# Bias and mask of the second block's attentions: from TensorE products to an operand of the instruction that finds the maximum

## The chip, the cores and the metric

The kernel runs on one core of a Trainium2 chip. The metric is the device time of one execution in microseconds (us). TensorE (PE) multiplies, VectorE (DVE) and ScalarE (ACT) work element by element and read TensorE's results from PSUM banks, GpSimd (POOL) works on SBUF only and issues the stores, SyncE (SP) issues the loads. Each engine runs its own list of instructions in order.

## The reference, cut to what matters

Two blocks act on 512 tokens of 1024 features: a first block with attentions and 32 experts, then a second block of two layers. A layer has three branches, a gated sum of their projections and an output projection. Two branches are attentions of eight heads. Of these the scores matter here:

```python
# latent attention (96 features of a head): a token sees its own chunk of 64 and the earlier ones
s = jnp.einsum('bqhd,bkhd->bhqk', qi, k) * scale
mask = key_chunk[None, :] <= q_chunk[:, None]
s = jnp.where(mask[None, None], s, NEG_INF)
p = jax.nn.softmax(s, axis=-1)
...
# banded attention (64 features): the same keys here, since the band is 9 chunks and there are 8, and a bias by distance
dist = i[:, None] + pad - j[None, :]
bias = rel_table[:, jnp.clip(dist, -REL_CLIP, REL_CLIP) + REL_CLIP]
s = jnp.einsum('bqhd,bkhd->bhqk', qi, kb) * scale + bias[None]
s = jnp.where(valid[None, None, None, :], s, NEG_INF)
p = jax.nn.softmax(s, axis=-1)
```

## The kernel before, in words

Products in float32 accuracy are made of three products of split operands (`mm3`, L61 to L63: high by low, low by high, high by high). The order of the instructions is not written out: the program is traced in the order of the code and a scheduler with a model of the engines' times then orders each engine's list, within what the buffers allow.

A layer of the second block is `layer2`. After the norm and the spatial gating unit come the latent and then the banded attention. Each goes over two halves of four heads, in a half over the four query tiles i of 128 tokens, and in a tile over two pairs of heads. Tile i sees n = 128 (i + 1) keys, so n is 128, 256, 384 or 512. After each pair one of 40 fillers is traced (`filler`: a feature tile of u, z or the gates, 24 products of 512 columns into the one bank F, then ScalarE or ScalarE and VectorE empty it and GpSimd stores it).

A pair is `unit2`. For each of its heads `S_of` leaves the scores in one of four banks M. Then VectorE takes their maximum (L1093, n elements) and multiplies it by -scale (L1094, one element), ScalarE takes exp(scale * s - scale * max) from the bank into an SBUF tile P with the sum (L1096), VectorE inverts the sum (L1098) and scales P (L1099). There are four buffers of P. TensorE transposes P (L1107, bank T), the result is split into Ph and Pl, and three products per key tile with the values give O.

Mask and bias are products that are accumulated in the same bank:

- in the latent attention L1321 adds `quad` (128 x 128, bf16, NEG in its first 64 rows and last 64 columns) to the last 128 columns by a product with the identity, between the three products of queries and keys (L1320, L1322, L1323);
- in the banded attention L1373 and L1375 add the low and the high part of the bias, as products of a matrix that reverses the rows (`rev`) with `rsl` and `rsh`, where row p holds the bias table from position p on, and L1374 adds `quad`; then `mm3` adds queries by keys.

There are 64 pairs, 128 heads: in each layer 32 heads of either kind, 8 of each n. The tables are made once in the first block (`bias_tables`, L173 to L189): 16 rows of 640, split and stored in DRAM as Rh and Rl (40 KB each). Each half of the banded attention loads its four heads' rsh and rsl from there, 256 KB a head and part.

Of the kernel before, what the change touches and what calls it, by code (L numbers as in the profile page):

```python
# [28 lines left out]
# slots of an expert's list in the main path  # L29
NS = 96  # L30
# weight tiles of the experts that are loaded ahead of the router
# [3 lines left out]
def f(t):  # L35
    return t.bitcast(F32)


class Kern:
# [6 lines left out]
    def split(self, hi, lo, src, scale=None, eng=None):  # L46
        """hi = src rounded to float32r, lo = src - hi (exact)."""
        nc = self.nc
        if scale is None:
            self.last_act = nc.scalar.activation(hi, src, AF.Copy)  # L50
            self.last_dve = (eng or nc.vector).tensor_sub(lo, src, f(hi))  # L51
        else:
            nc.scalar.activation(hi, src, AF.Copy, scale=scale)
            self.last_dve = nc.vector.scalar_tensor_tensor(lo, src, scale, f(hi), op0=ALU.mult, op1=ALU.subtract)

    def mm3(self, out, pairs, start=True, stop=True):
        """out += sum over pairs ((ah, al), (bh, bl)) of a.T @ b in float32 accuracy."""
# [7 lines left out]
    def rstd(self, pool, ss, n, scale, name):  # L65
        """1 / sqrt(ss * scale + EPS): a first value from the exponent's bits and two Newton steps,
        their constants set for the smallest largest error (5e-7)."""
# [21 lines left out]
    def weight(self, src, nk, ncol, pools=None, q=None, parts=1, plan=()):  # L89
        """src: AP [nk*128, ncol] in DRAM. Returns per k tile (hi, lo) APs [128, ncol].  # L90
        plan: for the first chunks, the pools, what the split is to come behind, and the engine of the remainders."""
# [4 lines left out]
        for k0 in range(0, nk, q):  # L96
# [10 lines left out]
            if early:  # L107
                # behind the router's work on each engine
# [15 lines left out]
    def bcast(self, ap, n):  # L124
        """DRAM vector [n] on all partitions."""
        return bass.AP(tensor=ap.tensor, offset=ap.offset, ap=[[0, 128], [1, n]])

    def norm_T(self, i, x, gain, xh, xl, pool, keep=None):
        """Tile i of x [128, D], token-major -> x * rstd * gain, transposed and split."""
# [18 lines left out]
    def setup(self, ctx):  # L148
# [17 lines left out]
        # reversal of the rows  # L166
        rev = self.rev = c.tile([128, 128], F32R, name="rev")
        # diagonal tiles of the second block: a query's own chunk and the earlier ones are open
        quad = self.quad = c.tile([128, 128], BF, name="quad")
        nc.gpsimd.memset(quad, 0.0)  # L170
        nc.gpsimd.memset(quad[0:64, 64:128], NEG)

    def bias_tables(self, pool):  # L173
        """Bias tables of the banded attention, reversed and extended, over the scale of the scores, split:
        R[m] = 8 * tab[min(639 - m, 256)]"""
        nc = self.nc
        self.R = R = [self.dram.tile([2, 8, 640], F32, name=f"R{s}") for s in "hl"]
# [6 lines left out]
        rh, rl = pool.tile([16, 640], F32R, name="rh"), pool.tile([16, 640], F32R, name="rl")  # L184
        nc.gpsimd.tensor_scalar(rx, rx, 8.0, None, op0=ALU.mult)
        nc.gpsimd.tensor_copy(rh, rx)
        nc.gpsimd.tensor_sub(rl, rx, f(rh))
        self.st(R[0].rearrange("l h n -> (l h) n"), f(rh))
        self.st(R[1].rearrange("l h n -> (l h) n"), f(rl))  # L189

# [1 line left out]
    def probs(self, banks, nh, nk, scale, m, s, normal=False):  # L192
        """banks: scores in psum, [128, nh, nk * 128] each. Leaves the maxima in m and the sums of the exponentials
        in s ([128, heads]); returns per pair of heads and key tile the exponentials, over their sums if normal,
        transposed: (hi, lo) rhs [128, 2 heads, 128]."""
# [34 lines left out]
    def values(self, vs, pr, dst):  # L230
        """Sum over key tiles of values.T @ probs for a pair of heads -> dst [128 (head, dim), 128], whole or (hi, lo)."""
# [10 lines left out]
    def rope_tables(self, pool, cosap, sinap, gain, nrot, name):  # L242
        """A = C * gain, B = Sg * gain with its halves swapped; cos/sin given for the first nrot dims."""
# [18 lines left out]
    def headnorm(self, ps, nh, A, B, nrot, out, i):  # L262
        """ps: psum [128, nh*64] -> per-head rmsnorm and rotation, into out [128, nh, 64]."""
# [3 lines left out]
        # copied, so that the bank is free early  # L267
# [29 lines left out]
    def block1(self):  # L297
# [37 lines left out]
        # fillers after each query tile of the groups and of the dense branch  # L335
# [3 lines left out]
        def bank():  # L339
            """A psum bank of either pool, in turn."""  # L340
# [4 lines left out]
        def filler(n=1):  # L345
            """Feature tiles of the gates, as tanh(z / 2) = 2 sigmoid(z) - 1, kept in DRAM until the merge."""
# [16 lines left out]
        # masks over key tiles (earlier, own, later): 0 where allowed, NEG elsewhere;  # L363
        # it[p, c] = c - p, key - query = c - p + 128 * rel
# [15 lines left out]
        t = self.tmp.tile([128, 128], F32, name="mt", bufs=1)  # L380
        nc.gpsimd.iota(t, pattern=[[1, 128]], base=-127, channel_multiplier=1, allow_small_or_imprecise_dtypes=True)
        nc.vector.tensor_scalar(self.rev, t, 0.0, None, op0=ALU.is_equal)
        # keys, transposed and zero-padded: [pair, head of the pair, key]
# [34 lines left out]
        def scores(qh, ql, p, v, s, j0, j1, mk):  # L418
            """Scores of head s of query pair p, key pair v over key tiles j0..j1."""
# [8 lines left out]
        def scores_b(qh, ql, p, s):  # L428
            """The same for the dense branch; both halves of the partitions hold the keys."""
# [5 lines left out]
        # dense grouped-query branch; its keys and the inputs of the projections take the place of the groups' keys  # L435
# [5 lines left out]
        def combine(i):  # L441
            """Joins the dilation groups: weights exp(scale * (m_g - M)) / sum."""
# [68 lines left out]
        def dilated(g, tr):  # L511
# [21 lines left out]
            for i in range(NT):  # L533
# [5 lines left out]
                # outputs of the 8 heads, their maxima, their sums  # L539
# [32 lines left out]
        # a branch's first keys are projected before the last query tile of the one before  # L572
# [13 lines left out]
        # gates, branch projections, merge, output projection  # L586
# [30 lines left out]
        # rows of the accumulator that empty slots are added to  # L617
# [6 lines left out]
        for c, W in enumerate(Ws):  # L624
            banks = [bank() for _ in range(NT)] if c == 0 else None
            if c == 0:
                # weights outermost, so that those of the second half take their place early
# [18 lines left out]
    def route(self, pool):  # L646
        """Norm, router, top 4, ranks of the tokens in their experts' lists. Returns the work for half a tile."""
# [10 lines left out]
        # slots, less BIG: what the rank of a chosen token is compared with  # L658
# [5 lines left out]
        # rows of the accumulator that empty slots are added to  # L664
# [6 lines left out]
        # router weights times the norm's gain, rounded | remainders  # L671
# [6 lines left out]
        # per token: its number, less BASE; per (token, expert): its gate, rounded and remainder  # L678
# [11 lines left out]
        def half(i, c, x):  # L690
# [46 lines left out]
            # the first expert's slots before anything else  # L737
# [4 lines left out]
            for i, lt, tv, sel in todo:  # L742
                # gates: softmax of the four
# [15 lines left out]
    def onehot(self, pool, e, eng):  # L759
        """Tokens of the slots of an expert, one-hot: [token, tile, slot]."""  # L760
# [5 lines left out]
    def slots(self, bank, oh, V, vg, gi, gate):  # L766
        """Token of each slot (a spare row of its own for an empty one) and its gate, in columns: the work of either."""
# [22 lines left out]
    def moe_setup(self):  # L790
        """Constants of the experts, and their pool of raw weights."""
# [10 lines left out]
        # biases of all experts, rounded in rows 0-31, remainders in rows 32-63, their second half in rows 64-127  # L802
# [19 lines left out]
    def moe_early(self):  # L822
        """First weights of the first expert."""
# [689 lines left out]
```

## Time and profile before

| | us |
|---|---|
| median of three runs | 3157.68 |
| lowest and highest | 3156.82, 3165.53 |
| span of the profiled execution, first to last instruction | 3154.3 |
| its TensorE busy | 3020.5 |
| its VectorE busy | 2233.5 |
| its ScalarE busy | 1712.6 |
| its GpSimd busy | 629.4 |

The profile is of one execution, whose span is 3.4 us below the median of the runs; no other time is given for it. Matmuls are pipelined, so the record of one begins before that of the one ahead has ended: how long TensorE is taken by one is read from the distance of two starts, not from the duration.

### The profile page before, as it was taken

The page shows a single profiled execution, that of the slowest core. Times are in us where ns is not written, and L with a number is a line of the kernel's source. Part 1 is how long each engine was busy: PE and PEld are TensorE (multiplying, and loading weights), DVE is VectorE, ACT ScalarE, POOL GpSimd, SP SyncE. Part 2 cuts the span into 40 slices and gives each one's busy share as a digit, 9 for nine tenths or more (in the row PEclk, how much of TensorE's full clock was granted, in tenths as well). Part 3 has the DMA queues.
Part 4 walks back from the last instruction along what each step waited for, and adds up shares of the span by engine and source line. Part 5 has one row for each costly group of instructions (what it writes and reads, how often), then busy time and mean ns, then how long its engine had stood idle before and what let it go on. Part 6 is the DMA issues. An engine that isn't in the chain of part 4 may idle for free. (4 is left out here: it accounts for less than half of the span.)

```text
span 3154.3 us, 40478 instructions
## 1 busy us (share of the span) xinstructions
PE 3020.5 (96%) x14662; PEld 2327.0 (74%) x14662; DVE 2233.5 (71%) x3715; ACT 1712.6 (54%) x2535; POOL 629.4 (20%) x438
## 2 busy tenths in 40 slices
PE   8999899979999999999999998999999979999998
PEld 6898777766666666666666665878887868888876
DVE  7766587668888988888888987644455585545564
ACT  4645554336776777777777774434444234444432
POOL 1000011033324444444444002111101010111000
PEclk9999999979999999999999998999999989999999
DMA  5122232569999999999999995433435433334362
GB/s 160 61 62 68 88 105 77 181 228 321 350 347 328 338 344 343 343 346 344 343 340 350 344 346 155 128 112 104 122 111 191 150 104 118 113 114 116 102 235 91
DMA packets 407761, 648.48 MB, mean 206 GB/s; under 512 B 23028, under 2 KB 150532, under 8 KB 407556
## 3 DMA queue, kind: packets, MB, share of 16 engines
q1 hardware_dynamic: 387808, 585.73, 55.6%
q0 software_dynamic: 19168, 58.00, 6.1%
q8 instruction: 118, 1.93, 0.3%
q10 hardware_dynamic: 576, 2.10, 0.2%
q14 instruction: 91, 0.71, 0.1%
HBM read 596.16 MB, written 53.79 MB: 206 GB/s over the span
## 5 line engine op out<-in xcount | busy, mean ns | idle before, releaser
L51 DVE TENSOR_TENSOR wlo<-raw,whi 128x2048 fp32r<-128x2048 f32 (+3 forms) x636 | 1157.7, 1831 | 318.6 <-ACT whi L50 314.3
L50 ACT ACTIVATE whi<-raw 128x2048 fp32r<-128x2048 f32 (+3 forms) x646 | 973.2, 1531 | 211.0 <-PE M L63 104.1
L61 PE MATMUL G<-wlo,exh 128*96 128x512 f32 x1024 | 412.8, 403 | 1.8 <-DVE wlo L51 1.8
L63 PE MATMUL G<-whi,exh 128*96 128x512 f32 x1024 | 404.0, 394 | 0.0
L62 PE MATMUL G<-whi,exl 128*96 128x512 f32 x1024 | 403.8, 394 | 0.0
L763 POOL TENSOR_SCALAR poh<-i,rk 128x96 fp32r<-128x96 f32 x124 | 314.4, 2545 | 94.1 <-PE T L779 94.0
L61 PE MATMUL F<-xl,whi 128*128 128x512 f32 x768 | 311.3, 405 | 14.5 <-DVE fl L1199 7.0
L62 PE MATMUL F<-xh,wlo 128*128 128x512 f32 x768 | 304.5, 396 | 1.8 <-DVE wlo L51 1.8
L63 PE MATMUL F<-xh,whi 128*128 128x512 f32 x768 | 304.6, 397 | 0.0
L61 PE MATMUL M<-wlo,xh 128*128 128x512 f32 (+2 forms) x736 | 277.5, 379 | 7.0 <-DVE wlo L51 2.0
L62 PE MATMUL M<-whi,xl 128*128 128x512 f32 (+2 forms) x736 | 276.9, 377 | 0.7 <-DVE xl L51 0.7
L63 PE MATMUL M<-whi,xh 128*128 128x512 f32 (+2 forms) x736 | 273.3, 373 | 0.0
L61 PEld LDWEIGHTS G<-wlo,exh 128*96 128x96 f32 x1024 | 165.5, 162 | 81.2 <-issue 18.2
L63 PEld LDWEIGHTS G<-whi,exh 128*96 128x96 f32 x1024 | 165.5, 162 | 70.4
L62 PEld LDWEIGHTS G<-whi,exl 128*96 128x96 f32 x1024 | 165.9, 162 | 64.2 <-issue 1.2
L61 PE MATMUL Y<-wlo,ath 128*96 128x512 f32 x512 | 210.2, 411 | 2.6 <-POOL wlo L51 1.9
L62 PE MATMUL Y<-whi,atl 128*96 128x512 f32 x512 | 202.1, 395 | 0.0
L63 PE MATMUL Y<-whi,ath 128*96 128x512 f32 x512 | 201.6, 394 | 0.0
L61 PEld LDWEIGHTS F<-xl,whi 128*128 128x128 f32 x768 | 145.3, 189 | 53.4 <-DVE fl L1199 11.2
L61 PEld LDWEIGHTS M<-wlo,xh 128*128 128x128 f32 x736 | 164.7, 224 | 26.3 <-ACT kk L269 4.4
L62 PEld LDWEIGHTS M<-whi,xl 128*128 128x128 f32 x736 | 164.8, 224 | 15.5 <-DVE xl L51 1.4
L63 PEld LDWEIGHTS M<-whi,xh 128*128 128x128 f32 x736 | 164.6, 224 | 14.2 <-issue 0.2
(480 smaller groups left out, 5413.7 us busy)
## 6 DMA issues: line engine op xcount, KB each, us to landing
raw<-in_w_gate_up SPq DMA_DIRECT2D x256, 1024.0 KB, 6.4
raw<-in_w_down SPq DMA_DIRECT2D x124, 1024.0 KB, 7.1
raw<-in_w_in SPq DMA_DIRECT2D x154, 512.0 KB, 3.9
GZ<-fl POOLq DMA_DIRECT2D x80, 256.0 KB, 2.3
raw<-in_w_out SPq DMA_DIRECT2D x24, 512.0 KB, 4.0
raw<-in_w_branch SPq DMA_DIRECT2D x24, 512.0 KB, 4.4
gt<-GZ SPq DMA_DIRECT2D x48, 256.0 KB, 3.1
raw<-in_w_in SPq DMA_DIRECT2D x32, 256.0 KB, 2.9
```

The costliest lines, as they stand in the source:

```text
L50: self.last_act = nc.scalar.activation(hi, src, AF.Copy)
L51: self.last_dve = (eng or nc.vector).tensor_sub(lo, src, f(hi))
L61: nc.tensor.matmul(out, lhsT=ah, rhs=bl, start=start and i == 0, stop=False)
L62: nc.tensor.matmul(out, lhsT=al, rhs=bh, start=False, stop=False)
L63: self.last_mm = nc.tensor.matmul(out, lhsT=ah, rhs=bh, start=False, stop=stop and i == n - 1)
L763: eng.tensor_scalar(oh[:, i], self.i128[:, :NS], self.rk[:, i, e:e + 1], None, op0=ALU.is_equal)
```

## The change

The products with `quad`, `rev` and the tables go. VectorE's first instruction on the scores becomes one that reads the bank and a tile of the same shape in SBUF, writes P = -scale * (scores + tile) and, as a second output, the smallest of each row; ScalarE then takes exp(min - P) in place. The tile is `quad`, now 128 x 512 in float32, for the latent attention, and `rb`, the bias with NEG written into its masked corner by GpSimd, for the banded one. So that row q of `rb` can be loaded as a shifted row, the table is stored with 128 copies of each of its 16 rows: 16 x 128 rows of 640 numbers, 641 apart, which are 5.24 MB. A half of the banded attention loads 4 x 256 KB instead of 8 x 256 KB, into two buffers instead of one.

```diff
     def bias_tables(self, pool):
-        self.R = R = [self.dram.tile([2, 8, 640], F32, name=f"R{s}") for s in "hl"]
+        R = self.R = self.dram.tile([16, 128 * 641], F32, name="R")
...
-        rh, rl = pool.tile([16, 640], F32R, name="rh"), pool.tile([16, 640], F32R, name="rl")
         nc.gpsimd.tensor_scalar(rx, rx, 8.0, None, op0=ALU.mult)
-        nc.gpsimd.tensor_copy(rh, rx)
-        nc.gpsimd.tensor_sub(rl, rx, f(rh))
-        self.st(R[0].rearrange("l h n -> (l h) n"), f(rh))
-        self.st(R[1].rearrange("l h n -> (l h) n"), f(rl))
+        self.st(R.rearrange("h (q m) -> h q m", m=641)[:, :, :640], rx[:, None, :].to_broadcast([16, 128, 640]))
...
-    def unit2(self, S_of, nk, vs, scale):
+    def unit2(self, S_of, bias, nk, vs, scale):
...
             src = S_of(h)
-            nc.vector.reduce_max(nm[:, h:h + 1], src[:, :n], axis=AX.X)
-            nc.vector.tensor_scalar(nm[:, h:h + 1], nm[:, h:h + 1], -scale, None, op0=ALU.mult)
             pt = self.ptile.tile([128, 512], F32, name="P2", bufs=4)
-            nc.scalar.activation(pt[:, :n], src[:, :n], AF.Exp, bias=nm[:, h:h + 1], scale=scale,
+            nc.vector.tensor_tensor_reduce(pt[:, :n], src[:, :n], bias(h), scale=-scale, scalar=3e38,
+                                           op0=ALU.add, op1=ALU.min, accum_out=nm[:, h:h + 1])
+            nc.scalar.activation(pt[:, :n], pt[:, :n], AF.Exp, bias=nm[:, h:h + 1], scale=-1.0,
                                  accum_out=sp[:, h:h + 1])
...
+        quad = self.quad = c2.tile([128, S], F32, name="quad")
+        nc.gpsimd.memset(quad, 0.0)
+        nc.gpsimd.memset(quad[0:64, 448:], NEG)
...
-                            nc.tensor.matmul(b[:, :n], lhsT=qh[:, g], rhs=kl[:, g, :n], start=True, stop=False)
-                            nc.tensor.matmul(b[:, n - 128:n], lhsT=self.ident_b, rhs=self.quad, start=False, stop=False)
-                            nc.tensor.matmul(b[:, :n], lhsT=ql[:, g], rhs=kh[:, g, :n], start=False, stop=False)
-                            nc.tensor.matmul(b[:, :n], lhsT=qh[:, g], rhs=kh[:, g, :n], start=False, stop=True)
+                            self.mm3(b[:, :n], [((qh[:, g], ql[:, g]), (kh[:, g, :n], kl[:, g, :n]))])
...
-                rs = [cp.tile([128, 4, 512], F32R, name=f"rs{s}") for s in "hl"]
-                for s in range(2):
-                    for h in range(4):
-                        row = tabs[s][l, 4 * hf + h]
-                        nc.sync.dma_start(f(rs[s])[:, h], bass.AP(tensor=row.tensor, offset=row.offset,
-                                                                  ap=[[1, 128], [1, 512]]))
+                rb = cw.tile([128, 4, 512], F32, name="rb")
+                for h in range(4):
+                    row = self.R[8 * l + 4 * hf + h]
+                    nc.sync.dma_start(rb[:, h], bass.AP(tensor=row.tensor, offset=row.offset + 127,
+                                                        ap=[[640, 128], [1, 512]]))
+                nc.gpsimd.memset(rb[0:64, :, 448:], NEG)
...
-                            nc.tensor.matmul(b[:, :n], lhsT=rev, rhs=rs[1][:, g, 512 - n:], start=True, stop=False)
-                            nc.tensor.matmul(b[:, n - 128:n], lhsT=self.ident_b, rhs=self.quad, start=False, stop=False)
-                            nc.tensor.matmul(b[:, :n], lhsT=rev, rhs=rs[0][:, g, 512 - n:], start=False, stop=False)
                             self.mm3(b[:, :n], [((qc[0][:, p, sl], qc[1][:, p, sl]),
-                                                 (kz[0][:, p, h, :n], kz[1][:, p, h, :n]))], start=False)
+                                                 (kz[0][:, p, h, :n], kz[1][:, p, h, :n]))])
```

The scheduler orders the lists anew. TensorE, first layer, start of the banded attention: M<-xl, M<-xh are the last products of the queries' projection, rsl, rsh, quad the products that go, kzc the keys, F a filler. Before:

```order
L63 MATMUL M<-xh_17952,whi 128x512
L1373 MATMUL M<-rsl,rev 128x128
L1374 LDWEIGHTS ident_b
L1374 MATMUL M<-quad,ident_b 128x128
L1375 MATMUL M<-rsh,rev 128x128
L61 MATMUL M<-kzcl,qch 128x128
L62 MATMUL M<-kzch,qcl 128x128
L63 MATMUL M<-kzch,qch 128x128
L1373 MATMUL M<-rsl,rev 128x128
```

Now:

```order
L63 MATMUL M<-xh_17942,whi 128x512
L61 MATMUL M<-kzcl,qch 128x128 x2
L62 MATMUL M<-kzch,qcl 128x128
L63 MATMUL M<-kzch,qch 128x128
L62 MATMUL M<-kzch,qcl 128x128
L63 MATMUL M<-kzch,qch 128x128
L63 MATMUL F<-xh_17942,whi 128x512
L61 MATMUL F<-xl_17943,whi 128x512
```

Three of a head's six products are gone, and a filler's products stand behind two heads' scores, where those of a third head followed.

VectorE, first layer, first two pairs of the latent attention (fl is a filler's, wlo a filler's weights). Before:

```order
L1199 SCALAR_TENSOR_TENSOR fl<-fl,F 128x512
L1093 TENSOR_REDUCE nm_18925<-M 128x1 x2
L1093 TENSOR_REDUCE nm_18999<-M 128x1 x2
L51 TENSOR_TENSOR wlo<-raw,whi 128x1024
L1094 TENSOR_SCALAR nm_18925<-nm_18925 128x1 x2
L1094 TENSOR_SCALAR nm_18999<-nm_18999 128x1 x2
L1098 RECIPROCAL sp_18926<-sp_18926 128x1
```

Now:

```order
L1193 SCALAR_TENSOR_TENSOR fl<-fl,F 128x512
L1084 ISA P_18921,nm_18915<-M,quad 128x128
L1084 ISA nm_18915 128x1
L1084 ISA P_18930,nm_18915<-M,quad 128x128
L1084 ISA nm_18915 128x1
L1084 ISA P_18991,nm_18985<-M,quad 128x128
L1084 ISA nm_18985 128x1
L1084 ISA P_19000,nm_18985<-M,quad 128x128
L1084 ISA nm_18985 128x1
L51 TENSOR_TENSOR wlo<-raw,whi 128x1024
L1088 RECIPROCAL sp_18916<-sp_18916 128x1 x2
```

The new instruction is listed as ISA, with the read of its second output as a row of its own, so a head still has two rows here; it writes P, and the split of the weights (wlo) now stands behind all of them.

GpSimd, first block, where the tables are made (r_i and r_pcol are the router's; the next rows are the experts' gathers and splits). Before:

```order
L185 TENSOR_SCALAR rx<-rx 16x640
L186 CAST rh<-rx 16x640
L187 TENSOR_TENSOR rl<-rx,rh 16x640
L188 DMA Rh<-rh 16x640
L189 DMA Rl<-rl 16x640
L657 IOTA r_i_6322 128x32
```

Now:

```order
L179 TENSOR_SCALAR rx<-rx 16x640
L180 DMA R<-rx 2048x1x640
L645 IOTA r_i_6309 128x32
```

Two small stores have become one of 2048 rows, in the same place.

## Rows read from the trace of the kernel before

**Rows 1.** The page's first line.

```profile
span 3154.3 us, 40478 instructions
```

**Rows 2.** First layer's latent, banded stretch: busy PE, PEld, DVE, ACT, POOL; PEclk, DMA.

```profile
2055.00:2250.00 195.00, 189.94 (x962) 155.50 (x963) 94.25 (x238) 84.85 (x192) 20.63 (x38) 0.99 0.38 108
2250.00:2400.00 150.00, 150.00 (x911) 130.37 (x910) 77.68 (x190) 67.87 (x164) 14.50 (x24) 1.00 0.36 107
```

**Rows 3.** Waits of TensorE, latent stretch 2055 to 2250: us, times, longest.

```profile
PE F L61 <- DVE fl L1199: 4.1, 5, 2.2
PE F L61 <- ACT fl L1201: 1.1, 2, 0.7
```

**Rows 4.** TensorE in order of time, banded, a head of 128 keys: start, duration.

```profile
2358.08 0.28 PE L1373 MATMUL M<-rsl,rev 128*128 128x128 f32 x1
2358.20 0.23 PE L1374 MATMUL M<-quad,ident_b 128*128 128x128 bf16 x1
2358.24 0.31 PE L1375 MATMUL M<-rsh,rev 128*128 128x128 f32 x1
2358.38 0.28 PE L61 MATMUL M<-kzcl,qch 128*128 128x128 f32 x1
```

**Rows 5.** The same, a head of 512 keys.

```profile
2390.20 0.40 PE L1373 MATMUL M<-rsl,rev 128*128 128x512 f32 x1
2390.43 0.23 PE L1374 MATMUL M<-quad,ident_b 128*128 128x128 bf16 x1
2390.47 0.47 PE L1375 MATMUL M<-rsh,rev 128*128 128x512 f32 x1
2390.78 0.39 PE L61 MATMUL M<-kzcl,qch 128*128 128x512 f32 x1
```

**Rows 6.** The same, latent attention, a head of 384 keys.

```profile
2213.06 0.23 PE L1321 MATMUL M<-quad,ident_b 128*128 128x128 bf16 x1
2213.10 0.42 PE L1322 MATMUL M<-kh,ql 96*128 96x384 f32 x1
2213.36 0.34 PE L1323 MATMUL M<-kh,qh 96*128 96x384 f32 x1
2213.53 0.33 PE L1320 MATMUL M<-kl,qh 96*128 96x384 f32 x1
```

**Rows 7.** VectorE's groups by shape, 2000 to 2500: busy us, mean ns, idle before.

```profile
L51 DVE TENSOR_TENSOR Pl<-T,Ph 128x512 fp32r<-128x512 f32 x32 | 21.3, 684 | 24.4 <-ACT Ph L50 24.3
L1093 DVE TENSOR_REDUCE nm<-M 128x1 f32<-128x512 f32 x16 | 10.7, 684 | 12.2 <-PE M L1323 10.1 <-PE M L63 2.1
L1094 DVE TENSOR_SCALAR nm<-nm 128x1 f32<-128x1 f32 x64 | 8.7, 144 | 0.4
```

**Rows 8.** ScalarE's groups by shape, the same stretch: from PSUM, from SBUF.

```profile
L1250 ACT ACTIVATE so<-T 128x512 f32<-128x512 f32 x4 | 2.4, 595 | 3.8 <-PE T L1248 3.0 <-DMA O<-so 0.9
L50 ACT ACTIVATE whi<-raw 128x512 fp32r<-128x512 f32 x2 | 1.3, 634 | 2.1 <-DMA raw<-in_mla_w_ukv 2.1
```

**Rows 9.** Line L1096 (exp), banded stretch 2250 to 2400: ScalarE's idle us, times.

```profile
  PE T L1107: 4.6, 4
```

**Rows 10.** Tile X, first 20 us: GpSimd's one store of 0.5 MB, issue to landing.

```profile
DMA to landing us min/median/max: 9.0/9.0/9.0
```

**Rows 11.** Stretches behind the tables' store, columns as in rows 2.

```profile
570.00:610.00 40.00, 40.00 (x178) 33.12 (x177) 26.59 (x36) 12.47 (x15) 1.88 (x5) 1.00 0.50 158
610.00:650.00 40.00, 40.00 (x203) 33.91 (x202) 19.18 (x36) 12.08 (x23) 0.00 (x0) 1.00 1.01 356
```

**Rows 12.** GpSimd in order of time, 540 to 720.

```profile
570.55 0.57 POOL L188 DMA_DIRECT2D Rh<-rh  x1
...
666.25 4.56 POOL L51 TENSOR_TENSOR wlo<-raw,whi 128x2048 fp32r<-128x2048 f32 x1 [94.36 <-ACT whi L50]
678.92 2.62 POOL L786 DMA_INDIRECT xg<-XN,gi  x1 [8.11 <-DVE gi L775]
```

**Rows 13.** GpSimd in order of time, start of the second block.

```profile
1930.56 0.53 POOL L964 DMA_DIRECT2D xr<-X  x1 [10.39 <-DVE yl L958]
```

More of the change, by code (lines that the diff above doesn't have):

```diff
@@ L165, in setup @@
         nc.vector.tensor_copy(self.ident_b, self.ident)
[L167 to L171, printed above, removed]
     def bias_tables(self, pool):
         nc = self.nc
-        self.R = R = [self.dram.tile([2, 8, 640], F32, name=f"R{s}") for s in "hl"]
+        R = self.R = self.dram.tile([16, 128 * 641], F32, name="R")
         rt = pool.tile([16, 257], F32, name="rt")
@@ L379, in block1 @@
         nc.vector.tensor_scalar(m4, t, 0.0, NEG, op0=ALU.is_gt, op1=ALU.mult)
-        t = self.tmp.tile([128, 128], F32, name="mt", bufs=1)
-        nc.gpsimd.iota(t, pattern=[[1, 128]], base=-127, channel_multiplier=1, allow_small_or_imprecise_dtypes=True)
-        nc.vector.tensor_scalar(self.rev, t, 0.0, None, op0=ALU.is_equal)
         kz = [kp.tile([128, 4, 2, S], F32R, name=f"kz{s}") for s in "hl"]
@@ L1326, in layer2 @@
                               for j in range(i + 1)]
-                        put(self.unit2(S_of, i + 1, v2, 96 ** -0.5), 1, 2 * hf + p, i)
+                        bias = lambda h: self.quad[:, 512 - n:]
+                        put(self.unit2(S_of, bias, i + 1, v2, 96 ** -0.5), 1, 2 * hf + p, i)
                         filler()
@@ L1334, in layer2 @@
                 nc.gpsimd.memset(f(t)[64:128, :, 0], 0.0)
-            tabs, rev = self.R, self.rev
             for hf in range(2):
-                rs = [cp.tile([128, 4, 512], F32R, name=f"rs{s}") for s in "hl"]
-                for s in range(2):
-                    for h in range(4):
-                        row = tabs[s][l, 4 * hf + h]
-                        nc.sync.dma_start(f(rs[s])[:, h], bass.AP(tensor=row.tensor, offset=row.offset,
-                                                                  ap=[[1, 128], [1, 512]]))
+                rb = cw.tile([128, 4, 512], F32, name="rb")
[4 more added lines that the diff above has]
+                nc.gpsimd.memset(rb[0:64, :, 448:], NEG)
                 qc = [cw.tile([128, 2, S], F32R, name=f"qc{s}") for s in "hl"]
@@ L1372, in S_of @@
                             g = 2 * p + h
-                            nc.tensor.matmul(b[:, :n], lhsT=rev, rhs=rs[1][:, g, 512 - n:], start=True, stop=False)
-                            nc.tensor.matmul(b[:, n - 128:n], lhsT=self.ident_b, rhs=self.quad, start=False, stop=False)
-                            nc.tensor.matmul(b[:, :n], lhsT=rev, rhs=rs[0][:, g, 512 - n:], start=False, stop=False)
                             self.mm3(b[:, :n], [((qc[0][:, p, sl], qc[1][:, p, sl]),
-                                                 (kz[0][:, p, h, :n], kz[1][:, p, h, :n]))], start=False)
+                                                 (kz[0][:, p, h, :n], kz[1][:, p, h, :n]))])
                             return b
                         v2 = [tuple(t[:, p * 128:p * 128 + 128] for t in vs[j]) for j in range(i + 1)]
-                        put(self.unit2(S_of, i + 1, v2, 0.125), 2, 2 * hf + p, i)
+                        bias = lambda h: rb[:, 2 * p + h, 512 - n:]
+                        put(self.unit2(S_of, bias, i + 1, v2, 0.125), 2, 2 * hf + p, i)
                         filler()
```

## The prediction

> **What bounds the kernel now.** I read the stretches of the second block first, then the waits inside them, then TensorE in order of time. In the first layer's banded attention TensorE is busy 150.00 of 150 us and in the latent attention 189.94 of 195, at a clock of 0.99 to 1.00, while VectorE is busy for about half of either stretch, ScalarE for less than half and the DMA engines for a little over a third [rows 2]; the second layer's two stretches repeat these within 1.2 us. So TensorE sets the pace there, and the fillers are what it does while a softmax is under way. The waits say the same: in the banded stretch TensorE waits for nobody, and in the latent stretch its waits come to 5.2 us, all of them for the one bank F to be emptied before the next filler [rows 3]. No wait of TensorE there is for a softmax.
>
> A busy share of 1 does not say how much a product costs, since the records overlap. A 512-column product lasts 0.40 us in the record, but the next one starts 0.23 us later [rows 5]. I therefore cost the removed products by the distances of starts.
>
> **The change part by part.**
>
> *The banded attention's products.* A head of 128 keys spends 2358.08 to 2358.38, which is 0.30 us, on the three products that go [rows 4], and a head of 512 keys 2390.20 to 2390.78, which is 0.58 us [rows 5]. In both, the quad product takes only 0.04 us itself, but the float32 product behind the bf16 one takes longer than its like (0.14 against 0.12 for 128 columns, 0.31 against 0.23 for 512). 64 heads, 16 of each n; with 256 and 384 on the line between the ends, the mean is 0.44 us. 64 x 0.44 = 28.2 us of TensorE.
>
> *The latent attention's quad.* 64 such products, one for each head, at 0.04 us each, and the product behind takes 0.26 us where its like of the same 384 columns takes 0.17 [rows 6]: 0.13 us together. Where the product behind is short there is little of that second part, as the 128 columns of the banded head show (0.02) [rows 4]. Bounds 0.04 and 0.13, I take the middle, 0.085: 5.4 us. Together TensorE loses 33.6 us of work in stretches where it does not pause. This is the main term.
>
> *The new instruction on VectorE.* No row shows it. It reads a bank and an SBUF tile and writes SBUF, as the split of Pl does, which takes 0.684 us for 512 columns; the maximum that it replaces takes 0.684 too, and the scaling of one element 0.144 [rows 7], about what I take for the read of the second output, which is a row of its own in the new list. So by the nearest rows VectorE's work is unchanged, and I take 0. A gain from fewer instructions is excluded, since there are two rows before and two after. The upper bound is an instruction at half rate, which adds up to 0.684 us for 512 columns, and by length 0.43 us for the mean head (320 columns); over 128 heads 55 us of VectorE, which has some 101 us idle in the latent and 72 in the banded stretch of each layer [rows 2].
>
> [...]
>
> *ScalarE reads SBUF in place of PSUM.* For 512 columns 0.634 instead of 0.595 us [rows 8]: at most 0.04 us x 128 = 5 us of ScalarE, hidden, since it is idle for over half of each stretch [rows 2]. Without that cover it would be 5 us.
>
> *P's buffer is now taken by VectorE.* Before, VectorE found the maximum whether or not one of the four P buffers was free, and ScalarE waited for the buffer: 4.6 us in 4 waits in the banded stretch, for transposes of an earlier pair [rows 9]. Now VectorE's instruction waits for it, and behind it on VectorE stand the splits of the fillers' weights (wlo) and of Pl, for which TensorE waits later. The chain behind such a wait is longer by the instruction and its read, 0.684 + 0.144 = 0.83 us. Four waits in each of two layers make 6.6 us if nothing covers it, and 0 if a filler (24 products at 0.23 us, 5.6 us) stands between. TensorE shows no wait from the four that there are now [rows 2], so I take 2 us, nearer to 0.
>
> *The fillers' bank.* In the latent stretch TensorE waits for F already [rows 3], and the quad products are part of what covers those waits. At worst these 5.4 us come back as wait; at best the new order covers the waits, 5.2 us a layer. I take 0.
>
> *The tables' store.* Two stores of 40 KB become one of 5.24 MB, issued at 570 us, where Rh was [rows 12]. The nearest row is the store of X: 0.5 MB in 9.0 us to landing, among other loads [rows 10], so ten times as much takes 90 us at that pace; at the 356 GB/s that the loads reach between 610 and 650 us it takes 14.7 us [rows 11]. It lands between 585 and 660 us. In the first 40 of these TensorE is busy throughout and half of the DMA engines' time is free [rows 11]. Behind the store on GpSimd's queue comes the first gather, at 678.92 us, later than either end [rows 12]. The loads of the first experts' weights fill 610 to 650 us; what the store takes from them delays them by at most 14.7 us, and the split that GpSimd takes its share of starts at 666.25 us [rows 12], which leaves 16 us. I take 0, and 14.7 us if that cover is gone.
>
> *What is left.* `quad`'s clearing now stands on GpSimd ahead of the loads of xr at the start of the second block; GpSimd then waits 10.39 us for VectorE before the last of these anyway [rows 13], and clearing takes less than 1 us. 32 loads of 256 KB fewer, and two copies fewer on GpSimd beside the tables: off every wait above. NEG into `rb`: GpSimd waits for the load, and is busy 14.50 of 150 us [rows 2].
>
> **The sum.** Span 3154.3 [rows 1] - 28.2 - 5.4 + 2 = 3122.7 us. The median of the runs lies 3.4 us above the span, so 3126 us. From one execution to another 0.3% (9.5 us) is about what this measurement can tell from no change.
>
> **The rivals.**
>
> *Half rate.* The new instruction takes up to twice as long. VectorE does not become the bound (55 us into over 300 us of idle time), but chains lengthen. In the latent stretch TensorE has no wait for a softmax now [rows 3] and twice as many fillers as in the banded one to put between; in the banded stretch the pairs follow each other more closely. There I charge one head of each of 32 pairs, since the second head's part runs beside ScalarE's work on the first: 32 x 0.43 = 14 us, 3140 us. For it: nothing in the trace, only that no row excludes it. Against: both nearest rows take the same 0.684 us.
>
> *The store holds up the loads.* All of the 14.7 us are lost, because the store is slow and the experts' first weights come late: 3141 us. For it: 5.24 MB from 16 partitions, and DMA share 1.01 between 610 and 650 us. Against: the 16 us of cover.
>
> [...] No row here shows a large store from 16 partitions.
>
> *Slower: VectorE stands still.* With P's buffers as VectorE's condition, its waits put the weights' splits off, and the fillers come late, so that TensorE loses its cover. It decides from 42 us on (33.6 and the 9.5 of the measurement, less rounding), which is 0.66 us for each of 64 pairs. ScalarE's present wait is 4.6 / 4 = 1.15 us; if every pair met one on TensorE it would be 64 x 1.15 = 74 us: 3157.7 - 33.6 + 74 = 3198 us. For it: the new list puts the split behind all of a pair's scores. Against: only 4 of 16 pairs of a stretch meet such a wait now.
>
> *It takes nothing away.* The products that go only filled time in which TensorE would have waited for fillers' weights: 3158 us. Against: no wait for weights in [rows 3], and the second block's products follow each other without gaps.
>
> **How the numbers follow.** Forecast 0.64 (its own range 3114, with the latent stretches' waits for F gone, to 3134, with the latent gain and 2.6 us more lost), half rate 0.12, the store 0.11, slower 0.07, nothing 0.06. The likeliest is 3126 us. The range from 3114 to 3142 takes in the forecast and the two middle rivals, 0.87 of the chance, less some 0.05 for their tails. Faster by over 0.3% is below 3148.2 us: those three less a tail of 0.03, so 0.84; the same 0.09, from "nothing" and that tail; slower 0.07.
>
> **What would show it.** The distance of starts in the banded attention falls to three products a head, and its stretch becomes some 14 us shorter in each layer, TensorE still busy all of it; the latent one 2 to 3 us shorter. The new instruction's row at 512 columns reads about 0.68 us, under half rate 1.2 or more. TensorE's waits for F stay near 5 us a layer, and no waits of PE for P, wlo or Pl appear. The stretch from 570 to 690 us keeps its length. The prediction is wrong if the second block's TensorE idles for a softmax, if the experts begin later by more than 5 us, or if the new order loses what the products gave.

## Result and the profile after

| | median, us | lowest to highest | ratio to before, 95% |
|---|---|---|---|
| before (same chip) | 3157.25 | 3150.23 to 3165.53 | |
| after | 3187.13 | 3186.81 to 3189.77 | 1.0096 [1.0079, 1.0113] |

The change made the kernel 30 us slower, where 32 us faster was forecast. The page's first line of the changed kernel answers to [rows 1]: the span grew by 31.0 us, with 592 instructions fewer.

```profile
span 3185.3 us, 39886 instructions
```

The time was lost in two places, at the end of the first block and behind the attentions. I read them in the order of the program.

**The end of the first block.** GpSimd in order of time, answering to [rows 12]: the store is issued 3.1 us later than Rh was, but the first gather comes 37.3 us later (716.22 for 678.92).

```profile
573.71 1.11 POOL L180 DMA_DIRECT2D R<-rx  x1 [0.30 <-POOL rx L179]
...
704.40 4.55 POOL L51 TENSOR_TENSOR wlo<-raw,whi 128x2048 fp32r<-128x2048 f32 x1 [129.30 <-DVE nt L77]
716.22 2.71 POOL L774 DMA_INDIRECT xg<-XN,gi  x1 [7.27 <-DVE gi L763]
```

The transfers of 560 to 650 us by issue (KB each, median us to landing): the store takes 54.8 us, and the one load of w_proj_b beside it 39.6 us, where it took 3.8 before. The gate loads gt look harmless by their median.

```profile
R<-rx POOLq DMA_DIRECT2D x1, 5120.0 KB, 54.8
gt<-GL SPq DMA_DIRECT2D x16, 256.0 KB, 4.4
raw<-in_w_proj_b SPq DMA_DIRECT2D x1, 512.0 KB, 39.6
```

Their slowest one does not. Here is tile gt from 560 to 660 us, first the kernel before, then the changed one:

```profile
DMA to landing us min/median/max: 2.5/3.2/4.0
DMA to landing us min/median/max: 2.9/4.4/42.1
```

TensorE's longest wait there hangs on this load, issued at 585.6 us. VectorE waits 20.5 us for gt before it empties a bank (mb), and TensorE waits 16.9 us for that bank; in this stretch TensorE's three waits of this kind come to 25.3 us. The weights w_proj_b had landed by 620.5 us.

```profile
627.81 0.69 DVE L593 SCALAR_TENSOR_TENSOR mb<-gt,M 128x512 f32<-128x512 f32 x1 [20.53 <-DMA gt<-GL]
628.55 0.79 PE L61 MATMUL M<-kzl,whi 128*128 128x512 f32 x1 [16.89 <-DVE mb L593]
```

The stretches of [rows 11]: TensorE falls from 40.00 us busy in each to 31.55 and 23.11. In the first the DMA engines are busy for 0.96 of the time and move 139 GB/s, where before 0.50 moved 158.

```profile
570.00:610.00 40.00, 31.55 (x125) 25.00 (x124) 8.40 (x11) 3.18 (x3) 4.07 (x6) 0.90 0.96 139
610.00:650.00 40.00, 23.11 (x90) 18.32 (x90) 19.04 (x27) 9.34 (x12) 0.00 (x0) 0.76 0.79 182
```

**The second block's attentions.** The second block starts 38.0 us later than before (first product of the gating unit at 2039.4, before 2001.4), so the windows of [rows 2] are read 38 us later. TensorE is as busy as it was, at a granted clock of 1.00.

```profile
2093.00:2288.00 195.00, 189.37 (x949) 157.75 (x950) 92.12 (x237) 85.42 (x190) 24.56 (x42) 1.00 0.39 110
2288.00:2438.00 150.00, 150.00 (x883) 131.25 (x881) 77.85 (x195) 74.55 (x171) 13.63 (x26) 1.00 0.35 106
```

A banded head of 512 keys, as in [rows 5]: three products 0.23 us apart and nothing ahead of them. The 0.58 us of the three others are gone.

```profile
2411.27 0.39 PE L61 MATMUL M<-kzcl,qch 128*128 128x512 f32 x1
2411.50 0.39 PE L62 MATMUL M<-kzch,qcl 128*128 128x512 f32 x1
2411.73 0.40 PE L63 MATMUL M<-kzch,qch 128*128 128x512 f32 x1
2411.97 0.39 PE L61 MATMUL M<-kzcl,qch 128*128 128x512 f32 x1
```

Yet the attentions did not become shorter. From the first product of the gating unit to the start of the last attention product the two layers take 405.8 and 403.2 us, before 407.6 and 402.9. What changed is what lies inside: 883 and 888 filler products, before 814 and 825. At 0.23 us each these 69 and 63 more make about 16 and 15 us in a layer, near the 16.8 that the forecast counted as gain.

VectorE's groups by shape, answering to [rows 7] (first layer; busy us, mean ns of one, idle before): the new instruction takes 686 ns for 512 columns, as the maximum did (684), and the read of its second output 83 ns, where the scaling took 144.

```profile
L51 DVE TENSOR_TENSOR Pl<-T,Ph 128x512 fp32r<-128x512 f32 x32 | 21.4, 686 | 17.2 <-ACT Ph L50 17.0
L1084 DVE DVE_READ_ACCUMULATOR2_ANT nm<- 128x1 f32 x64 | 5.3, 83 | 0.0
L1084 DVE CUSTOM_DVE_ANT_0 P<-M,quad 128x512 f32<-128x512 f32 x8 | 5.3, 686 | 10.3 <-PE M L63 10.3
L1084 DVE CUSTOM_DVE_ANT_0 P<-M,rb 128x512 f32<-128x512 f32 x8 | 5.2, 686 | 2.9 <-PE T L1097 2.9
```

**The merge behind the attentions.** TensorE in order of time around the first layer's last attention product: five products of a filler F are left, then 8.84 us of nothing, then the merge's first products (M<-yl, M<-yh). For this pause the profile names no releaser ("issue").

```profile
2445.17 0.28 PE L63 MATMUL O<-Ph,cvh 128*128 128x256 f32 x1
2445.29 0.40 PE L62 MATMUL F<-xh,wlo 128*128 128x512 f32 x1
...
2446.23 0.39 PE L63 MATMUL F<-xh,whi 128*128 128x512 f32 x1
2455.45 0.77 PE L61 MATMUL M<-yl,whi 128*128 128x512 f32 x1 [8.84 <-issue]
2456.02 0.63 PE L62 MATMUL M<-yh,wlo 128*128 128x512 f32 x1
2456.45 0.63 PE L63 MATMUL M<-yh,whi 128*128 128x512 f32 x1
```

The second layer shows the same (9.02 us at 3051.31), put down to a load of z. What the first pause waits for is seen on the other queues. SyncE's queue waits for the last attention product and then issues the merge's first load; VectorE waits for the loads and makes yl, which the first product reads (a row of the queue's own waits of 2430 to 2485 us, then the queue and VectorE in order of time):

```profile
SPq L1383 <- PE O L63: 2.8, 1, 2.8
...
2445.53 0.34 SPq L1383 DMA_DIRECT2D z<-GZ  x1
...
2448.98 0.69 DVE L1388 TENSOR_TENSOR z<-z,o 128x512 f32<-128x512 f32 x1 [6.78 <-DMA o<-O]
...
2454.56 1.47 DVE L54 SCALAR_TENSOR_TENSOR yl<-z,yh 128x512 fp32r<-128x512 f32 x2
```

This chain was there before the change too. From the start of the last attention product to that of the merge's first it took 9.2 us before and 10.3 after, but before TensorE had 26 filler products to run meanwhile:

```profile
2408.96 0.28 PE L63 MATMUL O<-Ph,cvh 128*128 128x256 f32 x1
...
2418.15 0.48 PE L61 MATMUL M<-yl,whi 128*128 128x512 f32 x1 [1.63 <-DVE yl L54]
```

Windows of the merge, columns as in [rows 2], first the kernel before, which had about three fillers left here (74 products, 48 of them between the merge's products):

```profile
2409.00:2429.00 20.00, 17.43 (x76) 13.48 (x75) 10.95 (x15) 7.98 (x12) 2.16 (x4) 1.00 0.96 343
2429.00:2449.00 20.00, 17.94 (x71) 14.10 (x70) 14.93 (x22) 7.43 (x10) 0.54 (x1) 0.91 0.90 304
```

and the changed one:

```profile
2445.00:2465.00 20.00, 8.57 (x30) 6.09 (x30) 10.59 (x16) 5.33 (x9) 1.08 (x2) 0.83 0.89 310
2465.00:2485.00 20.00, 18.65 (x74) 14.62 (x73) 16.70 (x24) 7.47 (x10) 0.00 (x0) 0.91 0.81 260
```

Look at the DMA share: in either kernel these 40 us are full of loads (0.81 to 0.96), those of z, o, u, the gates and the branch weights, for which the merge's products wait. Before, TensorE ran fillers meanwhile. After, it stood still, and the products behind the pause start 0.43 us apart for 2.6 us, in place of 0.23 (granted clock 0.83 over the 20 us).

So the theories to test: **A**, the store by itself costs the first block some 37 us; **D**, the new order spends in the attentions the fillers that had covered the merge, some 10 us a layer; against them that the first block lost its time to a new order of its lists (B), and that the new softmax is now the limit, so that what is not waited for at the merge is waited for in the attentions (E).

### The profile page after: what moved, and what is told of

The parts are those of the page before. It is cut to its first block, busy times and chain, and to the rows that moved or that the text cites. A ratio compares the mean times of both kernels' runs of the same rounds, so it can differ in the third digit from the quotient of the medians.

```text
span 3185.3 us, 39886 instructions
## 1 busy us (share of the span) xinstructions
PE 2999.8 (94%) x14406; PEld 2311.2 (73%) x14406; DVE 2220.3 (70%) x3714; ACT 1716.3 (54%) x2535; POOL 632.2 (20%) x438
```

## Experiments

Each kernel was run beside the kernel before on the same chip, whose medians were 3156.02 (e1 to e4), 3156.75 (e5 to e8) and 3156.64 us (e9 to e12). The changed kernel had its own before, 3157.25 us, so a difference of two kernels from different rounds can be off by about 1 us.

**e1, the store alone.**

```diff
 # kernel before, bias_tables
...
+        Rx = self.dram.tile([16, 128 * 641], F32, name="Rx")
+        self.st(Rx.rearrange("h (q m) -> h q m", m=641)[:, :, :640], rx[:, None, :].to_broadcast([16, 128, 640]))
```

> The kernel before with one thing added: the 5.24 MB store of the 16 rows in 128 copies, from the same 16 partitions at the same place of GpSimd's queue, into a tensor that nothing reads. Nothing of the second block changes. Theory A (the store itself holds up the loads of the first block's end, and that is the whole loss there): the gap opens between the store and the first gather as after the change, 35 to 40 us, so about 3157 + 37 = 3194 us. Rival B (the store only takes its bytes' share of the transfers, and the gap after the change comes from the new order of the lists): at most 14.7 us, 3157 to 3172 us. Rival C (the store is hidden): 3157 us.

Measured 3192.54 us, 1.0117 [1.01, 1.0134]: 36.5 us more, with nothing else changed. A holds, B and C fall. Its slowest gt landed in 40.7 us, as after the change. Its row of the transfers:

```profile
Rx<-rx POOLq DMA_DIRECT2D x1, 5120.0 KB, 55.1
```

**e2, the changed kernel with a small table.** The queries of the banded attention are kept in reverse order within a tile, which the transposes of P undo with a reversing matrix (`rev`).

```diff
...
-        self.st(R.rearrange("h (q m) -> h q m", m=641)[:, :, :640], rx[:, None, :].to_broadcast([16, 128, 640]))
+        self.st(R, rx)
...
-                    nc.sync.dma_start(rb[:, h], bass.AP(..., offset=row.offset + 127, ap=[[640, 128], [1, 512]]))
-                nc.gpsimd.memset(rb[0:64, :, 448:], NEG)
+                    nc.sync.dma_start(rb[:, h], bass.AP(..., offset=row.offset, ap=[[1, 128], [1, 512]]))
+                nc.gpsimd.memset(rb[64:128, :, 448:], NEG)
...
-                    self.split(qc[0][:, p], qc[1][:, p], ps)
+                    qr = ps.rearrange("p (t q) -> p t q", q=128)[:, :, ::-1]
+                    self.split(..., qr)
...
-                                        pts[h][:, (b + c) * 128:(b + c + 1) * 128], self.ident)
+                                        pts[h][:, (b + c) * 128:(b + c + 1) * 128], perm or self.ident)
...
```

> The changed kernel without the big store: the table is one store of 40 KB again. The queries of the banded attention are split in reverse order within each tile of 128, so that a row of the bias is a shifted row of the table, loaded from position p on as before the change, and the transposes of P use the reversing matrix in place of the identity, which puts the queries back. No product is added; NEG goes to the other 64 rows. Theory A (the store costs 37 us, the second block is as in the changed kernel): 3187 - 37 = 3150 us, the first gather near 679 us. Rival B (the first block lost its time to the new order): near 3187 us. If reading the bank backwards or loading overlapping rows is slow, some 5 us above A.

Measured 3154.37 us, 0.9993 [0.9984, 1.0003]: 32.8 us under the changed kernel, the first gather at 682.40, the slowest gt landed in 5.6 us. A holds. What is left of the change is worth 2 us: nearly all that the second block should have gained is still missing.

**e3, the big table from DRAM.**

```diff
 # changed kernel
+        R0 = self.dram.tile([16, 640], F32, name="R0")
+        self.st(R0, rx)
-        self.st(R.rearrange("h (q m) -> h q m", m=641)[:, :, :640], rx[:, None, :].to_broadcast([16, 128, 640]))
+        self.st(R.rearrange("h (q m) -> h q m", m=641)[:, :, :640], R0[:, None, :].to_broadcast([16, 128, 640]))
```

> The changed kernel, its table of 5.24 MB written from a 40 KB copy in DRAM in place of the 16 partitions of SBUF: the same bytes in the same 2048 rows, the same queue and place, one small store more ahead of it. Theory A1 (the 16 partitions are what makes the store slow, 54.8 us to landing): the store lands in 15 to 30 us and half or more of the 37 us come back, 3150 to 3168 us. Rival A2 (the number of rows and bytes sets it, whatever the source): it lands in some 50 us again and the time stays at 3180 to 3190 us. Second block as in the changed kernel under either.

Measured 3159.70 us, 1.001 [1.0001, 1.002]: 27 of the 33 us come back though the bytes and rows written are the same. The source of the store makes most of the difference, as A1 said; the slowest gt now landed in 21.8 us. That it is the number of partitions, and not SBUF as a source, was not tested: no run stores from more of them. Its row:

```profile
R<-R POOLq DMA_DIRECT2D x1, 5120.0 KB, 30.0
```

**e4, fillers kept for the merge.** In the changed kernel, big store and all:

```diff
         self.mm3(o, list(zip(vs, phl)))
+        self.last_o = self.last_mm.ins
...
-            filler(40)
+            with tc.issue_after(self.last_o):
+                filler(40)
```

> The changed kernel with its big store; the last 4 of the 40 fillers of each layer must stand behind the last product of the banded attention on TensorE, as 3 did by themselves before the change. Nothing else is told to move. Theory D (what the second block lost is cover at the start of the merge: there TensorE waited 9 us and 4 us more behind it in each layer, since no filler was left): the wait of 9 us goes in both layers and the time falls by 15 to 25 us, 3162 to 3172 us. Rival E (the softmax chain is now the limit, so that fillers kept back leave as many waits in the attentions): the wait at the merge goes, as much appears in the attentions, and the time stays within 5 us of 3187 us.

Measured 3166.14 us, 21.0 us under the changed kernel (1.0032 [1.0019, 1.0044]). D holds, E falls. The first 40 us of its first merge: busy again, at no lower a DMA share (0.92 and 0.88).

```profile
2428.00:2448.00 20.00, 17.96 (x73) 14.24 (x72) 9.94 (x14) 6.22 (x10) 1.61 (x3) 0.91 0.92 318
2448.00:2468.00 20.00, 20.00 (x88) 16.10 (x87) 13.34 (x20) 8.93 (x12) 1.08 (x2) 1.00 0.88 290
```

**e5, both remedies**, the edits of e2 and e4.

> The two remedies together: the table of 40 KB with the queries in reverse order (3154.4 us alone) and the last 4 fillers of each layer kept behind the last product of the banded attention (21.0 us faster than the changed kernel alone). Theory A and D (two separate losses, one in the first block and one at the two merges): they add, 3187.1 - 32.8 - 21.0 = 3133 us, 3129 to 3137, some 23 us under the kernel before. Rival (they share something, such as transfers that the smaller table takes away anyway): 3145 us or more.

Measured 3133.20 us, 0.9919 [0.9905, 0.9933], as the sum of the two said. It is faster than both kernels.

**e6, the kernel before without fillers at the merge.**

```diff
-            filler(4)
+            filler(8)
```

> The kernel before, with mask and bias as products still, and one number changed: 8 of the 40 fillers are traced ahead of the latent attention in place of 4, so that all are used up when the banded attention ends and none stands at the start of the merge. The work is the same. Theory D (fillers at the merge are cover worth some 9 us of wait and up to 8 us behind it in each layer, with or without the change): a wait of some 9 us opens at the start of both merges and the time rises by 15 to 30 us, to 3171 to 3186 us. Rival F (the wait at the merge belongs to the new softmax): within 5 us of 3156 us. Rival E (what is not waited for at the merge is waited for in the attentions): a wait at the merge, the time within 5 us of 3156 us, since the attentions get better filled.

Measured 3185.06 us, 1.008 [1.0063, 1.0096]: 28 us lost with the old softmax, its products and the same work. The pause at the merge has nothing to do with the new softmax (F falls), and what it loses does not come back in the attentions (E falls again). TensorE at the first merge:

```profile
2427.48 0.28 PE L63 MATMUL O<-Ph,cvh 128*128 128x256 f32 x1
2435.42 0.77 PE L61 MATMUL M<-yl,whi 128*128 128x512 f32 x1 [7.67 <-DVE yl L54]
```

**e7 and e8, each half of the change alone, on the kernel before.** e7 takes the latent products away (`mm3` alone, a 128 x 512 quad for VectorE) and leaves the banded attention as it was; e8 takes the banded ones, with e2's small table, and leaves the latent attention.

> The kernel before with the latent attention's half of the change alone: VectorE adds a 128 x 512 quad there; the banded attention keeps its products, its tables and its old softmax. In the new order three fillers of each layer still stand at the merge. The prediction's step (64 quad products of 0.085 us go, nothing else): 3156 - 5.4 = 3150.6 us. Rival G (TensorE already waits for the bank F in this stretch, and the products that go come back as such waits): 3156 us, with the waits for F some 2.5 us longer in each layer.

Measured 3166.95 us, 1.0031 [1.0022, 1.0041]: 10 us slower. Neither expectation foresaw that. Its merges have 65 and 72 filler products, not far from the 74 before, but 41 and 48 of them, where before has 26, stand ahead of the merge's first product.

> The kernel before with the banded attention's half of the change alone, on the table of 40 KB with the queries in reverse order; the latent attention keeps its quad products and old softmax. In the new order some 40 products, 1.7 fillers, stand at each merge. The prediction's step (28.2 us of products go, nothing else): 3156 - 28 = 3128 us. Theory D (the missing third of the cover, 1.3 fillers of 5.6 us, comes back at each merge as slower products, up to 8 us a layer): 3128 + 7 to 16 = 3135 to 3144 us. Rival (the new softmax itself is slow): 3150 us or more.

Measured 3158.83 us, 1.0006 [0.9995, 1.0016]: no gain, where D as I had put it said 3135 to 3144. The time lies where the rival, a slow softmax, had put it (3150 or more); this run does not tell them apart, e11 does. The trace speaks for D with its size put too small: with 41 filler products left, all ahead of the merge and none between its products, there is no first pause, but the next 20 us are worse than in the changed kernel (12.32 us busy, granted clock 0.64), so that over 40 us TensorE is busy for 27.3 us in this kernel and 27.2 in the changed one, with 11.9 us of waits for yl in the merge where before shows 3.7.

```profile
2407.00:2427.00 20.00, 15.01 (x63) 10.96 (x61) 9.66 (x13) 6.13 (x10) 1.62 (x3) 1.00 0.95 340
2427.00:2447.00 20.00, 12.32 (x32) 8.66 (x32) 14.79 (x23) 6.59 (x10) 0.00 (x0) 0.64 0.76 253
```

**e9 to e11, the reserve of e4 on three kernels**: the kernel before as a control, e7, and e8.

> Control: the kernel before, with mask and bias as products, and only the last 4 fillers of each layer kept behind the last product of the banded attention. In its own order 3 of them stand there already. Theory D (the reserve gives back what the change's new order had taken from the merge, and nothing to a kernel that has its fillers there): 3152 to 3162 us. Rival (keeping fillers back is a gain of its own, and the 23 us of the two remedies over the kernel before have nothing to do with the products that went): 3145 us or less.

Measured 3155.10 us, 0.9995 [0.9986, 1.0004]: to a kernel that has its fillers at the merge the reserve gives nothing.

> The latent half of the change alone (3167 us without the reserve), with the last 4 fillers of each layer kept behind the last product of the banded attention. Theory D (the latent half was slower only because its new order left the merge a filler short and put those that were left ahead of the merge's first products): the loss goes and the 4 to 5 us of quad products remain as a gain, 3149 to 3156 us. Rival G (the waits for the bank F in the latent stretch eat the gain): 3157 to 3162 us. Rival (the new softmax is itself slower): 3163 us or more.

Measured 3156.33 us, 0.9998 [0.9989, 1.0007]. The 10 us of e7 are gone, so they hung on where the fillers stand, but no gain stands behind them: the latent half is worth nothing. The time lies between the upper end of D's range and the lower of G's; the waits speak for G. TensorE's waits in the second layer's attentions (us, times, longest), first the control e9, then e10:

```profile
PE F L61 <- DVE fl L1200: 2.3, 5, 0.8
PE F L61 <- ACT fl L1202: 1.1, 2, 0.7
...
PE O L61 <- DVE Pl L51: 0.5, 1, 0.5
```

```profile
PE F L61 <- DVE fl L1210: 4.8, 5, 2.4
PE O L61 <- DVE Pl L51: 2.9, 3, 1.5
...
PE F L61 <- ACT fl L1212: 0.5, 2, 0.3
```

> The banded half of the change alone on the table of 40 KB (3159 us without the reserve), with the last 4 fillers of each layer kept behind the last product of the banded attention. Theory D (the 28 us of products went, and 18 us of waits a layer came at a merge that runs at the pace of its loads): the merge's waits fall to 4 us a layer, some 4 us a layer return in the attention, 3159 - 20 = 3139 us, 3134 to 3143. Rival (the banded softmax is the limit): 3150 us or more.

Measured 3132.21 us, 0.9924 [0.9911, 0.9938], 2 us under the expected range; the rival of a slow softmax falls, for e8 too: the banded half alone, with fillers at the merge, is as fast as both halves (e5), and worth 3155.10 - 3132.21 = 22.9 us against the control.

**e12, a fifth buffer of P** in e5 (`name="P2", bufs=5`).

> The two remedies together (3133 us) with five buffers of P in place of four; the order at the merges is the same. The prediction's term (VectorE's waits for a P buffer cost TensorE 2 us, bounds 0 and 6.6): 3127 to 3133 us. Rival H (the 27 us in which VectorE waits for P buffers, in order, put the fillers' weights off and are what keeps the attentions from the predicted gain): 3126 us or less, with the waits of VectorE for P gone and fewer waits of TensorE for F.

Measured 3131.44 us, 0.9912 [0.9898, 0.9925], which overlaps e5's interval and lies in the range of the prediction's term; H falls. It does not settle the term, for VectorE's waits for a P buffer did not go: behind transposes (T) they come to 15.9 us in the first layer's banded stretch, in e5 13.7, and to 11.2 in the second layer's attentions, in e5 13.4.

## Why the prediction was wrong, by its own steps

The prediction named three signs of being wrong. Two came: the experts began 37 us later, and the new order lost what the products gave. The attentions' stretches, which were to become shorter, did not.

**The sum's first step, "Together TensorE loses 33.6 us of work in stretches where it does not pause", is where it failed most instructively.** The products did go, and the distances of starts are those of the trace. But a time taken out of an unpaused stretch is a gain only if the work that follows is ready sooner. The fillers are a stock of 40 a layer, not a pace. With fewer products in the attentions the list reached into that stock earlier, some 65 filler products in each layer, and the merge, which waits for its loads with or without the change, had almost none left. I looked for waits of TensorE in the attentions, found none but those for the bank F, and never asked what covered the next stage. e4 puts this at 21.0 us, e5 against e2 at 21.2, e6 shows it without the change, and e9 shows that the reserve is no gain of its own. The rival "It takes nothing away" had the right kind of reason with a wrong place: it looked for the loss among the fillers' weights. (A slip in its reading of the waits changes nothing: beside [rows 3] the latent stretch has one wait of 0.2 us for a softmax.)

**The tables' store**, taken as 0 with a price of 14.7 us, cost 32.8 (e2) to 36.5 us (e1). Both bounds on its landing were fair, 14.7 and 90 us for a measured 54.8. The step that failed is the next one, on the loads of the experts' weights: "what the store takes from them delays them by at most 14.7 us". I let the store take its bytes' share, looked for the harm at those loads alone, and read TensorE's busy 40 us [rows 11] as cover. But the DMA engines were busy for 0.96 of the time at only 139 GB/s, and a gate load that TensorE's banks depended on within those 40 us landed in 42.1 us in place of 4.0 at most. The rival "The store holds up the loads" was right in kind, with less than half of the price.

5.24 MB from 16 partitions in 54.8 us is 96 GB/s; e3's store of the same bytes, which reads DRAM instead, landed in 30.0 us, which is 175 GB/s.

**The banded products** (28.2 us) brought 22.9 (e11 against e9). The two layers' attentions are 11.3 and 11.5 us shorter there, with the same 792 and 797 filler products inside; TensorE's waits in them rise from 12.1 to 16.0 us, which would be most of the 5.3 that are missing. **The latent quad** (5.4) brought nothing (e10 against e9, both within 0.1% of before). Here **the fillers' bank**, taken as 0, stood near its worst end: TensorE's waits for VectorE to empty F and to split Pl grow from 2.3 and 0.5 to 4.8 and 2.9 us in the second layer, in the first from 4.6 and 0.5 to 5.5 and 1.8. All its waits in both layers' attentions come to 12.1 us in e9 and 17.4 in e10, so the 5.4 us came back as waits. Both halves' shortfalls are read from waits; no run took the waits away.

**The new instruction** at 0 extra was right: 686 ns for 684, and 83 for 144. "Half rate", whose factor of two no row had shown, is out. **ScalarE's source** was right: exp takes 716 ns from SBUF for 512 columns, 688 from the bank. **P's buffer**: VectorE's wait is there (13.7 us, 7 times, in the first banded stretch of the changed kernel), TensorE shows none for P, as said; whether it costs 2 us stays open, since e12 did not remove it. "VectorE stands still" is out, although the time went up. **What is left**, clearing `quad` on GpSimd, took 0.53 and 0.14 us, as said.

The forecast put right: 3126 + 32.8 for the store + 21.0 at the merges + 5.3 and 5.4 for the two gains that fell short = 3190.5, and 3188 from the control's 3155.1 us in place of 3157.7; measured 3187.1. These terms are differences of runs, so the sum shows that they add up and no large one is missing. The 2 us for P's buffer are still in it, and no run shows them.

## What to carry to other kernels

Work that fills waits is a stock. Before pricing removed work as gain, follow the stock into the next stage and ask which wait it covers there, and whether it stands between that stage's products or only ahead of them. Price a transfer by what it does to the others that run beside it: the same bytes landed in 54.8 us from 16 partitions and in 30.0 from DRAM, and a load that is hidden when it lands in 4 us is not hidden at 42. Test the remedy on the kernel before too: the control e9 is what tells a repaired loss from a gain of its own.

## What the runs showed of the hardware

Beside a store of 5.24 MB from 16 partitions the mean busy share of the 16 DMA engines was 0.96 over 40 us at 139 GB/s, and another queue's 512 KB load took 39.6 us to land, without that store 3.8. After a pause of 8.84 us in the changed kernel's first merge TensorE's 512-column products started 0.43 us apart for 2.6 us, in place of 0.23. So this merge lost time twice, in the pause and in the products behind it. e8's merge had a granted clock of 0.64 in its second 20 us; in the same kernel with fillers between the merge's products (e11) TensorE's products start 0.43 us apart for 3.0 us behind a wait of 1.86 us, and from 2406 to 2440 us 0.23 to 0.24. No run tells the two costs apart. The reversed read of a bank in e2 cost nothing: the split of the queries takes 598 ns on ScalarE and 688 on VectorE, in the changed kernel 598 and 689.
